# A second down block that begins with two plain pairs, and squares that discard into PSUM banks

## The chip, the cores and the metric

The kernel runs on one core of one Trainium2 chip. The metric is the device time of one execution in microseconds: median of 3 runs before the change 1084.82 (1084.63 to 1085.21).

## The reference

A decoder layer on x of 256 tokens by 2048, all in fp32, and a final norm:

```python
u = rmsnorm(h, ln1_w[l])
proj = jnp.einsum('bsd,de->bse', u, w_in[l])
...
h = h + jnp.einsum('bse,ed->bsd', y, w_out[l])
u = rmsnorm(h, ln2_w[l])
ff = jax.nn.silu(jnp.einsum('bsd,df->bsf', u, w_ffn_gate[l])) * jnp.einsum('bsd,df->bsf', u, w_ffn_up[l])
h = h + jnp.einsum('bsf,fd->bsd', ff, w_ffn_down[l])
return rmsnorm(h, final_norm_w)
```

`y` holds the outputs of a gated linear recurrence (convolution, scan) and of a chunkwise retention. The last product, `ff` (256 x 5632) by `w_ffn_down` (5632 x 2048), and the norm behind it are where the change lies.

## The kernel before

**Products.** Every fp32 number is split into a high part and a low part in the format fp32r, and each product of two blocks is three matmuls (`three`, L683 to L685): high by high, high of the left by low of the right, low of the left by high of the right. In names a trailing `h` or `l` is the part: `ah`, `al` are the left operand (activations), `sh`, `sl` sums of activation blocks, `wh`, `wl` and `bh`, `bl` weights (1024 wide and 512 wide).

**Weights.** A piece of 128 x 1024 fp32 (512 KB) is loaded by SyncE (L641) into one of 7 buffers named `raw`. `split` then makes two instructions: ScalarE (ACT) casts it (`wh`, L123), VectorE (DVE) subtracts (`wl`, L124). The 1024-wide results go to 4 pairs of split buffers, the 512-wide ones to the pool of 60 activation tiles [128 x 512] (`act_tile`), which also holds `ah`, `al`, intermediate `part`, `n` and, in the kernel before, `junk`. A buffer is free again when its last reader is done.

**Pairs.** The product is tiled in blocks of 256 tokens by 1024 columns (two halves of 128 tokens, two halves of 512 columns: banks `c11`, `c12`, `c21`, `c22` of PSUM). The inner dimension runs in pairs of two 128-row pieces. A *plain* pair (`EIGHT`) has 8 products, 24 matmuls of 512 columns. A *summed* pair (`SEVEN`) has 7 products, 21 matmuls, into `c11`, `c12`, `c21` and the banks `p1`, `p5`, `p6`, `p7`; it needs four sums of weight pieces, which DVE adds in place (`add`, L661). A summed pair's weights come in this order: the 512-wide `bh`, `bl` of the first piece; the second piece 1024 wide; then, after L661, the first load's buffer as (`t1`, `t3`), and the second's as (`t2`, `t4`). I write 12S for a summed pair 12.

**Two down blocks.** The columns 0 to 1023 are the first down block (d = 0), 1024 to 2047 the second (d = 1), each with 22 pairs in the order of `ORDER_DOWN`; `SUMMED_DOWN` says which are summed. The last two pairs of the second block (20 and 21) are split into 512-wide `bh`, `bl`, and their products are ordered by bank (`tail`): one of `c22b`, then `c11`, `c12`, `c21`, the left half of `c22`, the rest of `c22b`. When the last product of a bank is issued, `post` runs: `p1` is copied (ACT, L930); after `p7` DVE makes `n`, `part` and four updates of the rows `htok` (L934, L923, L924); a finished `c` bank is added to its row (DVE, L945), and `down_post` (L976) squares the row on ACT with a running sum (L983), and DVE multiplies it by the norm's weight (L988). L962 and L967 add the row of the last bank into PSUM ahead of its end.

**Order.** A scheduler that estimates each instruction's time fixes the order on each engine when the program is built; on the chip an engine goes strictly down its list. TensorE's order in the tail of the second down block is written by hand (L676 on, `manual_schedule`). Loads run three pairs ahead. When the sums of pairs 12 and 19 are no longer read, GpSimd loads the rows of the second block's columns back (`rows_back`, L1119).

## Time and profile before

| | |
|---|---|
| median of the runs | 1084.82 us |
| profiled execution | 1085.53 us |
| its span | 1083.7 us |
| TensorE busy | 1072.3 us, 99% |
| DVE, ACT busy | 972.0 us, 666.9 us |
| second down block begins | 958.21 us |
| last matmul begins | 1075.61 us |

The span is the profiled execution without what lies around it. In the profile PE is TensorE, and a matmul of 512 columns is shown with a length of 0.39 us but issues every 0.227 us, since matmuls overlap. A row of the timeline reads: start, length, engine, line, operation, output, inputs, size, and in brackets the idle time of the engine just before, with what ended it. In a table by stretch the number ahead of the DMA share is the TensorE clock granted, as a share of full speed.

### The profile page before, as it was taken

What the parts mean: (1) busy time and instruction counts of PE and PEld (TensorE: products, weight loads), DVE (VectorE), ACT (ScalarE), POOL (GpSimd) and SP (SyncE); (2) the same over time, 40 slices, a digit from 0 to 9 for tenths busy, and PEclk for the clock granted to TensorE, in tenths of its full rate; (3) what the DMA queues carried; (4) which work ended last, traced back from release to release, by engine and by line L of the source; (5) the groups of instructions that cost most, each with busy time, mean ns of one, the idle gap of its engine ahead of it and who ended that gap; (6) DMA issues with size and microseconds to landing.
All of it is one profiled execution on the core that took longest, in us unless ns stands there. A gap on an engine that the chain in (4) does not pass through costs nothing.

```text
span 1083.7 us, 14591 instructions
## 1 busy us (share of the span) xinstructions
PE 1072.3 (99%) x5083; PEld 897.5 (83%) x5083; DVE 972.0 (90%) x1411; ACT 666.9 (62%) x951; POOL 56.5 (5%) x73
## 2 busy tenths in 40 slices
PE   9999999999999999999999999999999999999997
PEld 7888888888888888888888888888888888878886
DVE  7789889988878889989999999999999899999886
ACT  7756744468746676656656566565656666655463
POOL 0603230000000000000000000000000010000001
PEclk9999999999999999999999999999999999999998
DMA  9964574554557587677776777776777856557662
GB/s 328 351 211 154 176 252 168 181 176 165 185 194 236 188 306 277 227 242 247 257 269 229 250 262 238 265 269 227 251 249 228 273 170 219 194 174 240 208 214 78
DMA packets 71386, 244.62 MB, mean 226 GB/s; under 512 B 8208, under 2 KB 8592, under 8 KB 71312
## 3 DMA queue, kind: packets, MB, share of 16 engines
q1 hardware_dynamic: 68400, 236.34, 64.3%
q0 software_dynamic: 1472, 4.72, 1.3%
q10 hardware_dynamic: 1440, 2.62, 0.6%
q8 instruction: 40, 0.66, 0.2%
q14 instruction: 34, 0.28, 0.1%
HBM read 239.46 MB, written 4.19 MB: 225 GB/s over the span
## 4 chain that ended last, share of the span: by engine, by line
PE 94%; POOL 1%; DMA 1%; DVE 1%; issue 1%; ACT 1%; SPq 0%; POOLq 0%; ACTq 0%
PE c L683 22%; PE c L685 22%; PE c L684 22%; PE fm L194 10%; PE fm L196 5%; PE tm L174 2%; PE tm L176 2%; PE tm L175 2%; PE p L685 1%; PE p L684 1%; PE p L683 1%; POOL sumsq L310 1%; PE ft L868 1%; DMA raw<-in_w_lx 1%; DMA raw<-in_w_v 0%
## 5 line engine op out<-in xcount | busy, mean ns | idle before, releaser
L123 ACT CAST wh<-raw 128x1024 fp32r<-128x1024 f32 (+1 forms) x500 | 464.5, 960 | 321.6 <-PE c L685 127.3
L124 DVE TENSOR_TENSOR wl<-raw,wh 128x1024 fp32r<-128x1024 f32 (+1 forms) x500 | 543.1, 1114 | 73.0 <-ACT wh L123 71.2
L684 PE MATMUL c<-wl,ah 128*128 128x512 f32 x814 | 317.7, 390 | 0.0
L685 PE MATMUL c<-wh,al 128*128 128x512 f32 x814 | 314.9, 389 | 0.0
L683 PE MATMUL c<-wh,ah 128*128 128x512 f32 x814 | 276.8, 392 | 0.0
L683 PEld LDWEIGHTS c<-wh,ah 128*128 128x128 f32 x814 | 153.4, 188 | 31.8 <-ACT wh L123 0.3
L685 PEld LDWEIGHTS c<-wh,al 128*128 128x128 f32 x814 | 152.8, 188 | 31.7 <-DVE al L124 0.3
L684 PEld LDWEIGHTS c<-wl,ah 128*128 128x128 f32 x814 | 152.9, 188 | 31.3
L194 PE MATMUL fm<-u,wh 128*128 128x512 f32 x512 | 161.3, 396 | 0.0
L196 PEld LDWEIGHTS fm<-u,wl 128*128 128x128 f32 x512 | 96.0, 188 | 22.5
L196 PE MATMUL fm<-u,wl 128*128 128x256 f32 x512 | 100.9, 278 | 0.0
L661 DVE TENSOR_TENSOR raw<-raw,raw 128x512 f32<-128x512 f32 x118 | 81.1, 688 | 2.0
L661 DVE TENSOR_TENSOR raw<-raw 128x512 f32<-128x512 f32 x118 | 80.6, 686 | 1.1
L194 PEld LDWEIGHTS fm<-u,wh 128*128 128x128 f32 x512 | 78.3, 189 | 0.3
L684 PE MATMUL c<-wl,sh 128*128 128x512 f32 x194 | 75.2, 389 | 0.0
L685 PE MATMUL c<-wh,sl 128*128 128x512 f32 x194 | 74.0, 389 | 0.0
L683 PE MATMUL c<-wh,sh 128*128 128x512 f32 x194 | 68.7, 391 | 0.3 <-ACT sh L123 0.3
L175 PE MATMUL tm<-wl,u 128*128 128x512 f32 x128 | 48.8, 394 | 0.0
L176 PE MATMUL tm<-wh,u 128*128 128x512 f32 x128 | 48.5, 390 | 0.0
L174 PE MATMUL tm<-wh,u 128*128 128x512 f32 x128 | 47.1, 398 | 0.8 <-ACT u L298 0.8
L1119 POOL DMA_DIRECT2D htok<-kept_rows x8 | 4.3, 546 | 796.4 <-DVE wl L124 704.0
L683 PEld LDWEIGHTS c<-wh,sh 128*128 128x128 f32 x194 | 36.4, 188 | 8.2 <-ACT sh L123 0.7
(247 smaller groups left out, 1076.2 us busy)
## 6 DMA issues: line engine op xcount, KB each, us to landing
raw<-in_w_gu SPq DMA_DIRECT2D x216, 512.0 KB, 5.1
raw<-in_w_down SPq DMA_DIRECT2D x91, 512.0 KB, 4.8
raw<-in_w_out SPq DMA_DIRECT2D x34, 512.0 KB, 4.3
raw<-in_w_lx SPq DMA_DIRECT2D x16, 512.0 KB, 6.9
raw<-in_w_k SPq DMA_DIRECT2D x16, 512.0 KB, 3.5
raw<-in_w_q SPq DMA_DIRECT2D x16, 512.0 KB, 3.7
raw<-in_w_rg SPq DMA_DIRECT2D x16, 512.0 KB, 3.5
raw<-in_w_lg SPq DMA_DIRECT2D x16, 512.0 KB, 3.4
```

Source lines behind the costliest of these rows:

```text
L123: act.copy(out=dst_h, in_=src)
L124: v.tensor_tensor(out=dst_l, in0=src, in1=dst_h.bitcast(F32), op=ALU.subtract)
L174: pe.matmul(ps, ah, wh, start=first, stop=False)
L175: pe.matmul(ps, ah, wl, start=False, stop=False)
L176: pe.matmul(ps, al, wh, start=False, stop=last)
L194: pe.matmul(ps, wh, hl, start=n + i == 0, stop=False)
L196: pe.matmul(ps[:, :S], wl, hl[:, :S], start=False, stop=n + i == len(order) - 1)
L310: pool.tensor_tensor(out=sumsq, in0=sumsq, in1=sq, op=ALU.add)
L661: v.tensor_tensor(out=dst, in0=a, in1=b, op=ALU.add)
L683: pe.matmul(p, ah, bh, start=first, stop=False, skip_group_check=onto)
L684: pe.matmul(p, ah, bl, start=False, stop=False, skip_group_check=onto)
L685: pe.matmul(p, al, bh, start=False, stop=last, skip_group_check=onto)
```

## The change

Two edits. The four squares of the first down block no longer write to an activation tile: `down_post` gets the bank that L945 has just read (`gone`), and the square's values, which nothing reads (only the sum beside them is used), are written there. The second block's order now starts with two plain pairs, 0 and 1, and from the third place on every other pair is summed until 17S: before it was summed at every other place from the second. What is computed, and the number of instructions of each engine, stay as they were.

```diff
-ORDER_DOWN = (3, 4, 0, 5, 6, 1, 7, 8, 2) + tuple(range(9, 22)), (0, 12, 1, 19, 2, 5, 3, 7, 4, 9, 6, 11, 8, 13, 10, 15, 14, 17, 16, 18, 20, 21)
+ORDER_DOWN = (3, 4, 0, 5, 6, 1, 7, 8, 2) + tuple(range(9, 22)), (0, 1, 12, 2, 19, 3, 5, 4, 7, 6, 9, 8, 11, 10, 13, 14, 15, 16, 17, 18, 20, 21)
...
-                    down_post(cb, t, 0, 512)
+                    down_post(cb, t, 0, 512, gone=None if d else ps[c])
...
-    def down_post(cb, t, c0, cw, src=None):
+    def down_post(cb, t, c0, cw, src=None, gone=None):
...
-        j = act_tile("junk")
+        j = act_tile("junk") if gone is None else gone
         act.activation(out=j[:, :cw], in_=src, func=AF.Square, accum_out=ssq[:, t, n : n + 1])
```

With it the order on the engines changes from the second down block on, at three places that matter here. In all rows a name's last numbers count the tiles.

**ACT where the second down block begins.** Before: the cast of 12S's second piece (`wh_1967`), a square, the cast of its (`t1`, `t3`), three squares, the `bh` of 19S, the cast of 12S's (`t2`, `t4`), then pair 1.

```order
L123 CAST bh_1960_9165<-raw_1959_9163 128x512
L123 CAST wh_1967_9231<-raw_1966_9229 128x1024
L983 ACTIVATE junk_1962_9182,ssq_120<-htok_1826_8628 128x512
L123 CAST wh_1969_9239<-raw_1959_9163 128x1024
L983 ACTIVATE junk_1963_9197,ssq_120<-htok_1828_8632 128x512
L983 ACTIVATE junk_1964_9212,ssq_120<-htok_1827_8630 128x512
L983 ACTIVATE junk_1965_9227,ssq_120<-htok_1829_8634 128x512
L123 CAST bh_1984_9289<-raw_1983_9287 128x512
L123 CAST wh_1971_9243<-raw_1966_9229 128x1024
L123 CAST wh_1974_9249<-raw_1973_9247 128x1024
```

Now: the casts of pair 1, three squares into the banks, the cast of 12S's second piece, the last square, the `bh` of 19S, then 12S's (`t1`, `t3`) and (`t2`, `t4`).

```order
L123 CAST bh_1966_9233<-raw_1965_9231 128x512
L123 CAST wh_1960_9165<-raw_1959_9163 128x1024
L123 CAST wh_1963_9227<-raw_1962_9225 128x1024
L983 ACTIVATE c11_1665_7913,ssq_120<-htok_1826_8628 128x512
L983 ACTIVATE c12_1668_7925,ssq_120<-htok_1828_8632 128x512
L983 ACTIVATE c21_1667_7921,ssq_120<-htok_1827_8630 128x512
L123 CAST wh_1973_9267<-raw_1972_9265 128x1024
L983 ACTIVATE c22_1666_7917,ssq_120<-htok_1829_8634 128x512
L123 CAST bh_1986_9321<-raw_1985_9319 128x512
L123 CAST wh_1975_9275<-raw_1965_9231 128x1024
L123 CAST wh_1977_9279<-raw_1972_9265 128x1024
```

The squares moved behind pair 1's casts, write PSUM banks, and 12S comes one plain pair later.

**DVE at the same place, now**, from the low parts of pair 1's second piece on (the next two instructions are `wl` of (`t1`, `t3`) and the L661 that completes `raw_1972`):

```order
L124 TENSOR_TENSOR wl_1964_9228<-raw_1962_9225,wh_1963_9227 128x1024
L988 TENSOR_TENSOR htok_1826_8628<-htok_1826_8628,fw_1830_8639 128x512
L988 TENSOR_TENSOR htok_1828_8632<-htok_1828_8632,fw_1831_8641 128x512
L661 TENSOR_TENSOR raw_1965_9231<-raw_1965_9231 128x512
L988 TENSOR_TENSOR htok_1827_8630<-htok_1827_8630,fw_1830_8639 128x512
L124 TENSOR_TENSOR wl_1974_9268<-raw_1972_9265,wh_1973_9267 128x1024
L988 TENSOR_TENSOR htok_1829_8634<-htok_1829_8634,fw_1831_8641 128x512
L124 TENSOR_TENSOR bl_1987_9322<-raw_1985_9319,bh_1986_9321 128x512
L661 TENSOR_TENSOR raw_1965_9231<-raw_1965_9231,raw_1972_9265 128x512
L661 TENSOR_TENSOR raw_1985_9319<-raw_1985_9319 128x512
L661 TENSOR_TENSOR raw_1972_9265<-raw_1965_9231,raw_1972_9265 128x512
L661 TENSOR_TENSOR raw_1985_9319<-raw_1985_9319,raw_1992_9350 128x512
```

Before, 12S's first three L661 came ahead of all L988; now L988 stands between them.

**DVE and PE in the tail.** Before, DVE had the low parts of the last two pairs (eight `bl`) and L967 in this order:

```order
L124 TENSOR_TENSOR bl_2132_10005<-raw_2130_10002,bh_2131_10004 128x512
L124 TENSOR_TENSOR bl_2134_10009<-raw_2130_10002,bh_2133_10008 128x512
L124 TENSOR_TENSOR bl_2137_10039<-raw_2135_10036,bh_2136_10038 128x512
L124 TENSOR_TENSOR bl_2139_10043<-raw_2135_10036,bh_2138_10042 128x512
L924 TENSOR_TENSOR htok_2041_9571<-htok_2041_9571,part_2126_9990 128x512
L124 TENSOR_TENSOR bl_2142_10049<-raw_2140_10046,bh_2141_10048 128x512
L124 TENSOR_TENSOR bl_2144_10053<-raw_2140_10046,bh_2143_10052 128x512
L124 TENSOR_TENSOR bl_2147_10084<-raw_2145_10081,bh_2146_10083 128x512
L124 TENSOR_TENSOR bl_2149_10088<-raw_2145_10081,bh_2148_10087 128x512
L967 TENSOR_TENSOR c22_1978_9261<-c22_1978_9261,htok_2041_9571 128x512
```

Now there are the low parts of 17S's (`t2`, `t4`), two of pair 18, and `n`:

```order
L124 TENSOR_TENSOR wl_2114_9948<-raw_2108_9933,wh_2113_9947 128x1024
L124 TENSOR_TENSOR wl_2117_9954<-raw_2115_9951,wh_2116_9953 128x1024
L124 TENSOR_TENSOR wl_2120_9984<-raw_2118_9981,wh_2119_9983 128x1024
L934 TENSOR_TENSOR n_2127_10018<-p6_1990_9339,part_2126_10000 128x512
L923 TENSOR_TENSOR part_2128_10020<-n_2127_10018,p5_1989_9335 128x512
```

Four row updates later come these, and then L962:

```order
L923 TENSOR_TENSOR part_2130_10026<-part_2129_10023,p5_1989_9335 128x512
L124 TENSOR_TENSOR bl_2133_10035<-raw_2131_10032,bh_2132_10034 128x512
L124 TENSOR_TENSOR bl_2135_10039<-raw_2131_10032,bh_2134_10038 128x512
L924 TENSOR_TENSOR htok_2037_9570<-htok_2037_9570,part_2130_10026 128x512
L124 TENSOR_TENSOR bl_2138_10045<-raw_2136_10042,bh_2137_10044 128x512
L124 TENSOR_TENSOR bl_2140_10049<-raw_2136_10042,bh_2139_10048 128x512
L124 TENSOR_TENSOR bl_2143_10080<-raw_2141_10077,bh_2142_10079 128x512
L967 TENSOR_TENSOR c22_1970_9245<-c22_1970_9245,htok_2037_9570 128x512
L124 TENSOR_TENSOR bl_2145_10084<-raw_2141_10077,bh_2144_10083 128x512
```

Two of the eight `bl` (`bl_2123`, `bl_2125`) are done earlier, ahead of 17S's last parts; the other six now stand behind `n` and the row updates of 17S, and the last one also behind L967. On PE `c22b`'s first product moved up into 17S, and the tail begins with `c11` alone:

```order
L685 MATMUL c21_1971_9249<-wh_2119_9983,al_1911_8965 128x512
L683 MATMUL c11_1968_9237<-bh_2122_9989,ah_1933_9062 128x512
L684 MATMUL c11_1968_9237<-bl_2123_9990,ah_1933_9062 128x512
L685 MATMUL c11_1968_9237<-bh_2122_9989,al_1934_9063 128x512
L683 MATMUL c11_1968_9237<-bh_2134_10038,ah_1933_9062 128x512
L684 MATMUL c11_1968_9237<-bl_2135_10039,ah_1933_9062 128x512
L685 MATMUL c11_1968_9237<-bh_2134_10038,al_1934_9063 128x512
L683 MATMUL c11_1968_9237<-bh_2137_10044,ah_1941_9102 128x512
L684 MATMUL c11_1968_9237<-bl_2138_10045,ah_1941_9102 128x512
L685 MATMUL c11_1968_9237<-bh_2137_10044,al_1942_9103 128x512
L683 MATMUL c11_1968_9237<-bh_2144_10083,ah_1941_9102 128x512
L684 MATMUL c11_1968_9237<-bl_2145_10084,ah_1941_9102 128x512
```

Before, `c22b` came first in it:

```order
L685 MATMUL c21_1979_9265<-wh_2128_9998,al_1911_8965 128x512
L683 MATMUL c22b_2150_10093<-bh_2133_10008,ah_1933_9062 128x256
L684 MATMUL c22b_2150_10093<-bl_2134_10009,ah_1933_9062 128x256
L685 MATMUL c22b_2150_10093<-bh_2133_10008,al_1934_9063 128x256
L683 MATMUL c11_1976_9253<-bh_2131_10004,ah_1933_9062 128x512
L684 MATMUL c11_1976_9253<-bl_2132_10005,ah_1933_9062 128x512
L685 MATMUL c11_1976_9253<-bh_2131_10004,al_1934_9063 128x512
L683 MATMUL c11_1976_9253<-bh_2138_10042,ah_1933_9062 128x512
L684 MATMUL c11_1976_9253<-bl_2139_10043,ah_1933_9062 128x512
L685 MATMUL c11_1976_9253<-bh_2138_10042,al_1934_9063 128x512
```

From 17S's first use of its (`t2`, `t4`) low part to the use of `bl_2145` are 35 matmuls in the program now: four of 17S, 21 of pair 18, ten of the tail.

## The prediction

> **What bounds the kernel now.** I read the page first: the busy shares, then the chain that ended last.

> ```profile
> PE 1072.3 (99%) x5083; PEld 897.5 (83%) x5083; DVE 972.0 (90%) x1411; ACT 666.9 (62%) x951; POOL 56.5 (5%) x73
> PE 94%; POOL 1%; DMA 1%; DVE 1%; issue 1%; ACT 1%; SPq 0%; POOLq 0%; ACTq 0%
> ```

> TensorE sets the end. Both programs issue the same 5031 matmuls, so only time in which PE waits, or runs at a lower clock, can change. The second view is the waits of PE over the whole run (engine, line, what it waited for; total, times, longest):

> ```profile
> PE warm L116 <- DVE eps_t L109: 1.1, 1, 1.1
> PE tm L174 <- ACT u L298: 0.8, 1, 0.8
> PE p L684 <- DVE wl L124: 0.8, 1, 0.8
> PE p L683 <- ACT wh L123: 0.5, 1, 0.5
> PE c L683 <- ACT sh L123: 0.3, 1, 0.3
> ```

> The third is a table by stretch (PE, PEld, DVE, ACT, POOL busy; granted clock; DMA share; GB/s). Of the last 180 us before the end only one stretch loses anything, and the two `p` waits above lie in it.

> ```profile
> 940.00:960.00 20.00, 20.00 (x90) 16.56 (x89) 18.48 (x24) 8.85 (x9) 0.00 (x0) 1.00 0.72 246
> 960.00:980.00 20.00, 18.66 (x73) 14.40 (x72) 18.15 (x26) 10.64 (x18) 0.00 (x0) 0.91 0.39 126
> 980.00:1000.00 20.00, 20.00 (x90) 16.57 (x89) 18.14 (x21) 11.83 (x13) 2.12 (x4) 1.00 0.78 266
> ```

> The timeline of PE there (start, length, what; in brackets the idle time): the second down block begins at 958.21.

> ```profile
> 958.21 0.39 PE L683 MATMUL c<-wh,ah 128*128 128x512 f32 x1
> 965.69 0.39 PE L683 MATMUL p<-wh,sh 128*128 128x512 f32 x1
> 966.86 0.50 PE L684 MATMUL p<-wl,sh 128*128 128x512 f32 x1 [0.79 <-DVE wl L124]
> 968.65 1.00 PE L683 MATMUL p<-wh,sh 128*128 128x512 f32 x2 [0.45 <-ACT wh L123]
> 973.09 0.39 PE L684 MATMUL c<-wl,ah 128*128 128x512 f32 x1
> ```

> From 958.21 to 965.69 are 33 intervals: 0.2267 us each is the pace. From 965.69 to 973.09 are 16 intervals, 3.63 us at that pace; they took 7.40. **3.77 us are lost.** Four intervals end at 968.65: 2.96 − 0.91 = 2.05 lost until then, waiting; the other 1.72 is the clock, below. Who is late:

> ```profile
> 956.41 1.05 ACT L123 CAST wh<-raw 128x1024 fp32r<-128x1024 f32 x1 [0.59 <-PE c L685]
> 963.62 0.63 ACT L983 ACTIVATE junk<-htok 128x512 f32<-128x512 f32 x1 [6.16 <-PE c L684]
> 964.25 1.04 ACT L123 CAST wh<-raw 128x1024 fp32r<-128x1024 f32 x1
> 967.55 4.03 ACT L123 CAST wh<-raw 128x1024 fp32r<-128x1024 f32 x4
> 961.19 0.68 DVE L661 TENSOR_TENSOR raw<-raw 128x512 f32<-128x512 f32 x1
> 964.38 0.69 DVE L988 TENSOR_TENSOR htok<-htok,fw 128x512 f32<-128x512 f32 x1 [1.06 <-ACT junk L983]
> 965.59 1.22 DVE L124 TENSOR_TENSOR wl<-raw,wh 128x1024 fp32r<-128x1024 f32 x1
> ```

> ACT stood 6.16 us before the square of L983, waiting for PE: its output `junk` takes an activation tile that PE was still reading for pair 0. The casts of 12S (S marks a summed pair) queue behind it, and DVE's L988 and `wl` behind those. PE starved on exactly these.

> **The clock.** The granted clock fell with the wait:

> ```profile
> 968.00:969.00 1.00, 0.55 (x2) 0.30 (x2) 1.00 (x3) 1.00 (x2) 0.00 (x0) 0.96 0.95 352
> 969.00:970.00 1.00, 1.00 (x4) 0.79 (x3) 1.00 (x2) 1.00 (x2) 0.00 (x0) 0.50 0.29 115
> 972.00:973.00 1.00, 1.00 (x5) 0.85 (x4) 1.00 (x2) 0.00 (x0) 0.00 (x0) 0.83 0.88 287
> 1078.00:1079.00 1.00, 0.00 (x0) 0.00 (x0) 0.90 (x3) 0.97 (x2) 0.00 (x0) 0.58 0.61 213
> 8.00:9.00 1.00, 0.82 (x4) 0.34 (x2) 0.00 (x0) 0.56 (x1) 0.00 (x0) 1.00 0.69 221
> 9.00:10.00 1.00, 0.35 (x2) 0.31 (x3) 0.91 (x3) 0.96 (x4) 0.00 (x0) 1.00 0.86 283
> ```

> A clock of 0.96 over one microsecond that is either full or half means half from 968.92; 0.83 means full again from 972.34. So 3.42 us ran at half speed: 1.71 us of PE work lost, which with the 2.05 makes up the 3.77. After the last matmul the clock falls at 1078.16, 109.24 us later, which is 32 × 3.414: I take it that the clock is decided at fixed steps of about 3.41 us. The step before 968.92, with 2.05 idle, brought half clock; 0.18 + 0.65 = 0.83 idle at 8 to 10 us did not.

> **The change, part by part.** *The squares.* They now write the PSUM bank that L945 has just read; DVE and ACT order is kept by waits, and the next block's `p1`, `p5` to `p7` need banks first after two plain pairs, 48 × 0.2267 = 10.9 us in, when the squares (four of 0.63) are long done; that work covers them. PSUM as ACT's output costs no more, by the groups of lines (busy, mean ns):

> ```profile
> L811 ACT COPY c<-q 128x512 f32<-128x512 f32 x13 | 7.6, 586 | 7.0 <-DVE q L810 7.0
> L808 ACT COPY p<-c 128x512 f32<-128x512 f32 x13 | 7.5, 576 | 1.6 <-PE c L685 1.6
> ```

> 586 into PSUM against 576 out of it. Term: 0.

> *The new beginning.* Pairs 0 and 1 are plain and PE reads them for 10.9 us. DVE works without a wait from 961.19: three 1024-wide `wl` and ten 512-wide operations stand before the L661 that releases the cast of 12S's last weights (t2, t4). Their pace comes from rows quoted next: (3.50 − 1.22)/2 = 1.14 and (2.49 − 0.68)/3 = 0.60. So that L661 starts at 961.19 + 3.42 + 6.03 = 970.64, takes 0.69, ACT follows 0.13 later (964.25 to 964.38 above is such a handover), and PE can use the cast 1.10 after its start (967.55 to 968.65): 972.56. PE asks for it at 958.21 + 63 × 0.2267 = 972.49. Loss 0.07. **Saved: 3.70.** If ACT or DVE loses a microsecond there, PE loses it too; the cover is thin.

> *The tail.* One plain pair fewer follows the last summed pair, 17S. The rows:

> ```profile
> 1030.99 4.63 DVE L124 TENSOR_TENSOR wl<-raw,wh 128x1024 fp32r<-128x1024 f32 x4 [0.59 <-ACT wh L123]
> 1041.72 3.50 DVE L124 TENSOR_TENSOR wl<-raw,wh 128x1024 fp32r<-128x1024 f32 x3 [0.60 <-ACT wh L123]
> 1062.90 2.49 DVE L124 TENSOR_TENSOR bl<-raw,bh 128x512 fp32r<-128x512 f32 x4
> 1065.31 0.69 DVE L967 TENSOR_TENSOR c<-c,htok 128x512 f32<-128x512 f32 x1
> 1067.97 0.69 DVE L945 TENSOR_TENSOR htok<-c,htok 128x512 f32<-128x512 f32 x1 [1.10 <-PE c L685]
> 1044.05 0.39 PE L684 MATMUL p<-wl,sh 128*128 128x512 f32 x1
> 1064.67 0.28 PE L683 MATMUL c22b<-bh,ah 128*128 128x256 f32 x1
> 1064.79 0.28 PE L684 MATMUL c22b<-bl,ah 128*128 128x256 f32 x1
> 1067.32 0.39 PE L684 MATMUL c<-bl,ah 128*128 128x512 f32 x1
> 1067.55 0.39 PE L685 MATMUL c<-bh,al 128*128 128x512 f32 x1
> ```

> Now: the last `bl` starts at 1062.90 + 1.81 = 1064.71. A 1024-wide `wl` started at 965.59 is used at 966.86, 1.27 later, so a 512-wide one 1.27 − 0.54 = 0.73 later: 1065.44. PE asks for it at 1067.32: 1.88 early.

> After: call N the moment when PE uses 17S's t2 (`p6`, L684). DVE prepared that weight a lead earlier than needed. In the kernel before, 15S has 1041.72 + 1.27 = 1042.99 against 1044.05: lead 1.06. To 17S DVE needs another round like 1030.99 to 1041.72, 10.73 (same rows of work: four `wl`, `bl`, and so on), while PE has 42 × 0.2267 + 3 × 0.12 = 9.88, since c22b's first product moved in there. Lead at 17S: 0.21, and nothing hides the rest. Then DVE does, in this order: `wl` of 17S, two `wl` of pair 18, `n`, five row updates, two `bl`, one more update, three `bl`, L967, the last `bl`. `n` starts at N − 1.27 − lead + 3 × 1.14 = N + 2.15 − lead; 13 × 0.60 later comes the last `bl`, ready 0.73 after that: N + 10.68 − lead. PE asks for it 35 intervals after N: 7.93. **Wait: 2.75 − lead, 2.5 with 0.21.** Bounds: 2.75 at lead 0; below, `n` can't start before `p6` is complete, 0.23 + 0.42 (1067.55 to 1067.97) after N, which leaves 0.65 + 7.80 + 0.73 − 7.93 = 1.25. I take 2.5, next to the row. It falls in three pieces: the second and fourth `bl` come late too, then the last one, which has L967 ahead of it, about 1.7.

> *Half clock after it.* That wait lies within 4 us, its largest piece in one step. The idle share of a step is thus about 1.7, between 0.83 (no loss) and 2.05 (loss), nearer to the latter. I take the loss, 1.71; other end 0.

> [...]

> **Sum**: −3.70 + 2.5 + 1.71 = +0.51, and 1085.53 becomes 1086.04. What follows PE's last product (row updates, norm, stores) is the same work in the same order and only shifts. The median of the runs, 1084.82, is 0.71 below the profiled run: **1085.3**.

> **Rivals.**
> *A, clock stays at full speed after the tail's wait*: 1085.3 − 1.7 = 1083.6. For it: no piece is longer than about 1.7. Against it: 968 to 972.
> *B is the forecast.*
> *C, the tail waits less*: DVE reaches 17S early, so only the 1.25 remains, too little for the clock: −2.45, 1082.4; with no wait at all 1081.1. For it: 15S's lead of 1.06 and 1.88 us of slack now. Against it: the order of DVE's work in the program.
> *D, slower: the supply of weights starves PE all through the block.* A summed and a plain pair cost PE 45 × 0.2267 = 10.20, DVE's round 10.73, since a load waits for the `wl` that frees its buffer. With 0.5 short in each of eight rounds, and 1.06 of lead to spend, 3.2 are lost, and the lead at 17S is 0: −3.70 + 3.2 + 2.75 + 1.71 = +4.0, 1088.8. It decides from the point at which the starving costs over 1.7. Against it: the kernel before runs the same rounds with a lead of 1.06 left at the seventh.
> *E, the change doesn't do what it says*: another item in ACT's queue (19S's `bh`, which takes pair 0's tile) holds it up as the square did; 1085.3 + 3.7 = 1089.0. Its cast stands ahead of 12S's t-casts, but pair 0's tile is free at about 963.6, before DVE gets that far.

> **Chances**: B 0.46, A 0.26, C 0.16, D 0.10, E 0.02. A measurement of this kernel can tell about 0.2%, 2.2 us, from no change. C is faster (0.16, and a little of A: 0.17); A and B within; D, E and a little of B slower (0.13). B alone gives 1084.3 to 1085.9; the range from C's 1082.4 to 1086.8 (starving of 1.5) leaves out C's better half, most of D, and E, under 2 in 10.

> **What would show it.** PE's waits lose both `p` rows of before, and the clock row at 969 reads 1.00. New rows stand near 1062 to 1066, PE `c` L684 waiting for DVE `bl` L124, in pieces of 0.2 to 1.7, total 2.5; then the clock reads 0.50 for 3.4 us. If the tail shows no such wait, the order of DVE was misread; if `p` L683 waits in every round between 980 and 1055, D holds; if waits for ACT `wh` stay near 968, E.

## The result, and the profile after

The changed kernel takes 1086.57 us (median of 20 runs, 1084.93 to 1087.96) against 1084.86 (20 runs, 1083.69 to 1085.5): ratio 1.0017, 95% interval 1.001 to 1.0024, so slower by 0.1 to 0.24%. The forecast was 1085.3, range 1082.4 to 1086.8. The time lies within, near the upper end; the way there was in part another than forecast.

The profiled execution took 1086.56 us, span 1084.8. Both profiles hold 5083 matmuls (the prediction's 5031 is in neither). PE's waits over the whole run, those of the second down block:

```profile
PE c L684 <- DVE bl L124: 1.7, 2, 1.4
...
PE p L683 <- ACT wh L123: 0.6, 1, 0.6
...
PE c L683 <- ACT wh L123: 0.4, 2, 0.2
```

Both waits of before at the block's beginning are gone. In their place stand waits for `bl` (the tail) and new ones for `wh`. The table by stretch says where:

```profile
960.00:980.00 20.00, 20.00 (x89) 16.31 (x88) 18.71 (x24) 9.56 (x14) 0.00 (x0) 1.00 0.48 154
...
1000.00:1020.00 20.00, 19.79 (x87) 15.65 (x86) 16.11 (x18) 9.43 (x11) 0.00 (x0) 1.00 0.58 186
1020.00:1040.00 20.00, 19.15 (x81) 14.61 (x80) 17.12 (x20) 10.88 (x12) 0.00 (x0) 1.00 0.53 182
...
1060.00:1080.00 20.00, 15.37 (x74) 11.99 (x72) 16.23 (x39) 8.27 (x21) 4.15 (x5) 1.00 0.15 53
```

960 to 980 loses no busy time now (before 1.34, and clock 0.91). 1000 to 1040 does, where before PE was busy throughout, as these two rows of the kernel before show:

```profile
1000.00:1020.00 20.00, 20.00 (x90) 16.56 (x89) 17.41 (x20) 10.27 (x12) 0.00 (x0) 1.00 0.60 192
1020.00:1040.00 20.00, 20.00 (x90) 16.55 (x89) 16.61 (x19) 10.54 (x12) 0.00 (x0) 1.00 0.61 206
```

Now the clock reads 1.00 in every one of these stretches, in the tail too. PE's timeline at the block's ends and at the pieces that cost, in the changed kernel:

```profile
957.47 0.39 PE L683 MATMUL c<-wh,ah 128*128 128x512 f32 x1
...
971.84 0.73 PE L683 MATMUL p<-wh,sh 128*128 128x512 f32 x2
...
1004.17 0.96 PE L683 MATMUL c<-wh,ah 128*128 128x512 f32 x3 [0.21 <-ACT wh L123]
...
1025.44 0.50 PE L683 MATMUL p<-wh,sh 128*128 128x512 f32 x1 [0.56 <-ACT wh L123]
...
1026.39 0.96 PE L683 MATMUL c<-wh,ah 128*128 128x512 f32 x3 [0.21 <-ACT wh L123]
...
1065.90 0.50 PE L684 MATMUL c<-bl,ah 128*128 128x512 f32 x1 [0.24 <-DVE bl L124]
...
1068.31 0.50 PE L684 MATMUL c<-bl,ah 128*128 128x512 f32 x1 [1.44 <-DVE bl L124]
...
1076.77 0.28 PE L685 MATMUL c22b<-bh,al 128*128 128x256 f32 x1
```

From the block's first product to its last are 512 intervals. Before they took 1075.61 − 958.21 = 117.40 us, of which 3.76 is lost against the pace; now 1076.77 − 957.47 = 119.30, of which 5.66 is lost. Laying each start against the pace of 0.2267 us gives the pieces: 0.2 at the beginning (971.8 to 972.4), 2.5 in the tail (1064.7 to 1068.7), and 3.0 in the rounds between, of which 1.6 near 1025. So the block lost 1.90 us more than before. In this execution it also began 0.74 us earlier, from differences at the very start of the run; hence the end is only 1.16 later in the two profiles, while the medians differ by 1.71.

### The profile page after: what moved, and what is told of

It is laid out like the page before. It is cut to its first block, busy times and chain, and to the rows that moved or that the text cites. A ratio compares the mean times of both kernels' runs of the same rounds, so it can differ in the third digit from the quotient of the medians.

```text
span 1084.8 us, 14590 instructions
## 1 busy us (share of the span) xinstructions
PE 1072.3 (99%) x5083; PEld 895.0 (83%) x5083; DVE 972.4 (90%) x1411; ACT 666.3 (61%) x951; POOL 55.8 (5%) x73
## 4 chain that ended last, share of the span: by engine, by line
PE 87%; DVE 5%; DMA 4%; ACT 2%; POOL 1%; issue 1%; SPq 0%; ACTq 0%; POOLq 0%; DVEq 0%
PE c L685 20%; PE c L684 20%; PE c L683 20%; PE fm L194 10%; PE fm L196 5%; DMA raw<-in_w_down 3%; PE tm L174 3%; PE tm L176 3%; PE tm L175 3%; DVE wl L124 2%; DVE raw L661 2%; POOL sumsq L310 1%; PE ft L868 1%; ACT wh L123 1%; DVE bl L124 1%
## 5 line engine op out<-in xcount | busy, mean ns | idle before, releaser
L123 ACT CAST wh<-raw 128x1024 fp32r<-128x1024 f32 (+1 forms) x500 | 463.4, 960 | 320.1 <-PE c L685 116.2
L124 DVE TENSOR_TENSOR wl<-raw,wh 128x1024 fp32r<-128x1024 f32 (+1 forms) x500 | 543.5, 1116 | 70.5 <-ACT wh L123 69.0
L684 PE MATMUL c<-wl,ah 128*128 128x512 f32 x814 | 317.7, 390 | 0.0
L685 PE MATMUL c<-wh,al 128*128 128x512 f32 x814 | 314.9, 389 | 0.0
L683 PE MATMUL c<-wh,ah 128*128 128x512 f32 x814 | 276.3, 392 | 0.5 <-ACT wh L123 0.4
L683 PEld LDWEIGHTS c<-wh,ah 128*128 128x128 f32 x814 | 152.3, 188 | 33.5 <-ACT wh L123 2.6
L685 PEld LDWEIGHTS c<-wh,al 128*128 128x128 f32 x814 | 152.8, 188 | 31.8 <-DVE al L124 0.3
L684 PEld LDWEIGHTS c<-wl,ah 128*128 128x128 f32 x814 | 152.8, 188 | 31.4
L661 DVE TENSOR_TENSOR raw<-raw,raw 128x512 f32<-128x512 f32 x118 | 81.1, 688 | 1.9
L661 DVE TENSOR_TENSOR raw<-raw 128x512 f32<-128x512 f32 x118 | 80.8, 687 | 1.1
L684 PE MATMUL c<-wl,sh 128*128 128x512 f32 x194 | 75.2, 389 | 0.0
L685 PE MATMUL c<-wh,sl 128*128 128x512 f32 x194 | 74.0, 389 | 0.0
L683 PE MATMUL c<-wh,sh 128*128 128x512 f32 x194 | 68.7, 391 | 0.3 <-ACT sh L123 0.3
L174 PE MATMUL tm<-wh,u 128*128 128x512 f32 x128 | 46.6, 394 | 0.6 <-ACT u L298 0.5
L683 PEld LDWEIGHTS c<-wh,sh 128*128 128x128 f32 x194 | 36.4, 188 | 8.2 <-ACT sh L123 0.7
```

What stands on the lines that cost most here:

```text
L123: act.copy(out=dst_h, in_=src)
L124: v.tensor_tensor(out=dst_l, in0=src, in1=dst_h.bitcast(F32), op=ALU.subtract)
L174: pe.matmul(ps, ah, wh, start=first, stop=False)
L661: v.tensor_tensor(out=dst, in0=a, in1=b, op=ALU.add)
L683: pe.matmul(p, ah, bh, start=first, stop=False, skip_group_check=onto)
L684: pe.matmul(p, ah, bl, start=False, stop=False, skip_group_check=onto)
```

## The experiments

**Which of the two edits does it?** `squares_only` has the first edit with the old order, `order_only` the second with activation tiles for the squares.

```diff
 squares_only, against the changed kernel:
-ORDER_DOWN = ..., (0, 1, 12, 2, 19, 3, 5, 4, 7, 6, 9, 8, 11, 10, 13, 14, 15, 16, 17, 18, 20, 21)
+ORDER_DOWN = ..., (0, 12, 1, 19, 2, 5, 3, 7, 4, 9, 6, 11, 8, 13, 10, 15, 14, 17, 16, 18, 20, 21)
 order_only, against the changed kernel:
-        j = act_tile("junk") if gone is None else gone
+        j = act_tile("junk")
```

> The first edit alone: the four squares discard into the PSUM banks, the order of the second down block is that of the kernel before. Theory (the order does the work): the 6.16 us wait of ACT before L983 goes, but 12S still follows after only one plain pair (24 products, 5.4 us), and DVE has the same row updates, low parts and sums to do before 12S's (t1, t3) and (t2, t4); PE still waits there, now for DVE, about 1.4 and 1.2 us in two pieces, and the rounds behind it start with no lead and starve by 0.3 us or more each. Time 1085 to 1088, not faster than before. Rival (the square's wait for a tile was the whole cause): the 3.77 us go and nothing comes, 1081.1.

> The second edit alone: the order with two plain pairs first, the squares still write activation tiles. Theory (the order does the work): with pair 1 after pair 0 the squares and casts find free tiles in time and PE loses 0.1 us at the boundary, as in the changed kernel; the tail's wait of 2.5 us and the starving of the rounds by about 2.7 us stay: 1086 to 1087.5, not told apart from the changed kernel. Rival (the square's tile is the cause): ACT waits again at L983, PE loses 2 to 3.8 us more, 1088.5 to 1090.5.

Measured: `squares_only` 1089.09 us, ratio 1.0044 (1.0031 to 1.0058); `order_only` 1086.46, ratio 1.0017 (1.0007 to 1.0026). PE's timeline in `squares_only`, and the cast that ended the second of these waits:

```profile
967.80 0.50 PE L684 MATMUL p<-wl,sh 128*128 128x512 f32 x1 [1.12 <-DVE wl L124]
969.53 0.91 PE L683 MATMUL p<-wh,sh 128*128 128x512 f32 x2 [1.00 <-ACT wh L123]
...
968.44 3.99 ACT L123 CAST wh<-raw 128x1024 fp32r<-128x1024 f32 x4 [2.49 <-DVE raw L661]
...
993.93 0.50 PE L683 MATMUL p<-wh,sh 128*128 128x512 f32 x1 [1.16 <-ACT wh L123]
```

The square's wait for a tile is gone in `squares_only`, and PE waits at the same place all the same, now for DVE's work: its `wl`, and its L661 ahead of the cast at 968.44. With the clock it loses 4.3 us against the pace there, and 2.0 more at 994. So the 3.77 us of before were not the square's alone: with one plain pair ahead of 12S there is not enough time for DVE. `order_only` can't be told from the changed kernel, and its profile loses only 0.5 us at the beginning: with two plain pairs first, the tiles for the squares are free in time. The order is the change; beside it the first edit is worth nothing measurable here, and alone it is a loss. For `squares_only` even the theory's range (1085 to 1088) was too low: it left out the clock, which halved behind that wait in the profiled execution, as in the profile of the kernel before (table by stretch of `squares_only`):

```profile
970.00:971.00 1.00, 1.00 (x4) 0.82 (x3) 1.00 (x2) 1.00 (x2) 0.00 (x0) 0.50 0.16 62
```

**The tail.** `pair17_plain` gives the tail a plain pair more by making pair 17 plain; `two_behind` takes the end of the old order, with 15S directly behind 13S.

```diff
 pair17_plain, against the changed kernel:
-SUMMED_DOWN = (9, 12, 15, 17, 19), (5, 7, 9, 11, 12, 13, 15, 17, 19)
+SUMMED_DOWN = (9, 12, 15, 17, 19), (5, 7, 9, 11, 12, 13, 15, 19)
 two_behind, against the changed kernel:
-... 10, 13, 14, 15, 16, 17, 18, 20, 21)
+... 10, 13, 15, 14, 17, 16, 18, 20, 21)
```

> The changed kernel with pair 17 plain instead of summed (one product more, 3 matmuls, 0.68 us; four sums of DVE fewer). Theory (the tail's wait comes of too little PE work behind the last summed pair's row updates): 15S is the last summed pair, with 16, 17 and 18 plain behind it, 72 matmuls, 16 us of cover; the waits for DVE bl, 2.5 us, go; the starving of the rounds up to 15S stays: 1086.5 - 2.5 + 0.7 = 1084.7, 1083.5 to 1085. Rival (the last pairs' loads or casts are late by themselves): the wait stays, 1087.2.

> The changed kernel with the end of the order of the kernel before (10, 13S, 15S, 14, 17S, 16, 18, 20, 21): two plain pairs again behind 17S, and in exchange 15S directly behind 13S. Theory: the waits for DVE bl (2.5 us) go; between 13S and 15S PE has 21 matmuls less cover (a plain pair is 5.4 us), so a new wait of 1 to 2 us for ACT wh stands near 1040; the starving before it stays: 1084.5 to 1086. Rival (the wait in the tail is not of the order): it stays, and the new wait adds to it, 1088.

Measured: `pair17_plain` 1084.1 us, ratio 0.9996 (0.9987 to 1.0005); `two_behind` 1086.34, ratio 1.0019 (1.001 to 1.0028). In neither is a wait for `bl` left. What `two_behind` gains in the tail it pays near 1040:

```profile
1042.11 0.50 PE L683 MATMUL p<-wh,sh 128*128 128x512 f32 x1 [1.74 <-ACT wh L123]
...
1043.05 0.96 PE L683 MATMUL c<-wh,ah 128*128 128x512 f32 x3 [0.22 <-ACT wh L123]
```

That is 2.5 us against the pace, above the 1 to 2 expected, and the time is 0.3 above the theory's range. Seven of the 11 runs have a mean clock of 0.996; the profiled one has 0.998, and its clock did not halve before PE's end. The tail's wait is DVE's list behind 17S, as the prediction had it: give PE a second plain pair behind the last summed pair and it goes.

**GpSimd for low parts.** If DVE's list is the matter, another engine could take some of it. In `pool_tail` GpSimd subtracts four of the last two pairs' eight `bl`; in `pool_b11` the first low part of every summed pair; in `pool_both` all of these.

```diff
 def split(dst_h, dst_l, src, by=None):
     act.copy(out=dst_h, in_=src)
-    v.tensor_tensor(out=dst_l, ...)
+    (by or v).tensor_tensor(out=dst_l, ...)
...
 pool_tail, pool_both: the second half of a load of the last two pairs
+    split(*self.parts[name], raw[:, n * 512 : n * 512 + 512], pool if n == 1 else None)
 pool_b11, pool_both: the first part of a summed pair of the second down block
+    split(*self.parts["b11"], r[:, :512], pool if self.last else None)
```

> The changed kernel with the second low part of each load of the last two pairs (four of the eight bl, the last one among them) subtracted by GpSimd instead of DVE. Theory (the tail's wait is DVE's list behind n): three operations of 0.60 us leave DVE's list ahead of PE's last need and the last bl no longer stands behind L967; the waits for DVE bl, 2.5 us with what they drag along, fall under 0.5, the starving of the rounds stays: 1083.5 to 1084.7. Rival (the wait is for the loads or the casts of the last pairs): no gain, 1086.6, or slower, since GpSimd takes about 1.3 us for what DVE does in 0.60.

> As pool_tail, and the first low part (b11) of every summed pair of the second down block is also made by GpSimd. Theory (the rounds starve because DVE's list holds the low part of the next summed pair, whose load is late, ahead of the sums and splits that PE needs first): DVE no longer stops for the load, its round falls from 10.6 us to 10.2 or less, the waits of PE for ACT wh between 1000 and 1040 go: 1081 to 1082.5, faster than both kernels. Rival (the loads or DVE's amount of work limit the round, wherever the low part stands): the waits stay, no better than pool_tail, 1083.5 to 1084.7.

> The changed kernel with the first low part of every summed pair of the second down block made by GpSimd, the tail left to DVE. In the two runs before, an all-SBUF operation of DVE took up to 2.1 us instead of 0.69 while GpSimd subtracted. Theory (starving comes of DVE stopping for the next summed pair's load; GpSimd gives part of it back by slowing DVE): the waits between 1000 and 1040 fall from 2.7 us to 1.0 to 1.5, the tail's 2.5 us stay: 1084.5 to 1086. Rival (nothing but the amount of DVE work or the loads counts): no less starving, 1086.5 or more.

Measured: `pool_tail` 1085.57 us, ratio 1.0015 (1.0006 to 1.0023); `pool_both` 1085.6, 1.0012 (1.0004 to 1.0021); `pool_b11` 1088.0, 1.0033 (1.0021 to 1.0044). All three are slower than their theories said. The timelines of GpSimd, DVE and PE in `pool_tail` say why:

```profile
1059.02 4.61 POOL L124 TENSOR_TENSOR bl<-raw,bh 128x512 fp32r<-128x512 f32 x3 [6.46 <-ACT bh L123]
...
1060.16 1.28 DVE L923 TENSOR_TENSOR part<-n,p 128x512 f32<-128x512 f32 x2
1061.37 2.81 DVE L924 TENSOR_TENSOR htok<-htok,part 128x512 f32<-128x512 f32 x2
...
1066.63 0.50 PE L684 MATMUL c<-bl,ah 128*128 128x512 f32 x1 [1.40 <-DVE bl L124]
```

While GpSimd subtracts (1059.02 to 1063.63), DVE's two L923, which read one operand from PSUM, take 1.28, as in the changed kernel; the two L924, both operands in SBUF, take 2.81 instead of the changed kernel's 1.29 and end at 1064.18, just after GpSimd does. DVE loses 1.5 of the 1.8 us that it was spared. In `pool_both` the same two pairs took 1.29 and 2.82.

`pool_b11` fails for a second reason: the first sum (L661) overwrites the piece that GpSimd still reads, and DVE waits for it instead of for the load:

```profile
1028.44 0.69 DVE L661 TENSOR_TENSOR raw<-raw,raw 128x512 f32<-128x512 f32 x1
1030.65 0.69 DVE L661 TENSOR_TENSOR raw<-raw 128x512 f32<-128x512 f32 x1 [1.52 <-POOL bl L124]
```

So it moved the stop of DVE but did not take it away. In its profile the loss between 1000 and 1060 did fall, from 2.9 us against the pace to 1.3, but half clock behind the tail's wait (below) takes as much again: the block loses 5.6 us in all, as in the changed kernel. Why the median is some 1.5 us above the changed kernel's is not explained by that.

**The rounds.** In the changed kernel, DVE and ACT ahead of the worst starving, at 1025:

```profile
1013.56 4.63 DVE L124 TENSOR_TENSOR wl<-raw,wh 128x1024 fp32r<-128x1024 f32 x4 [0.60 <-ACT wh L123]
1020.60 0.69 DVE L124 TENSOR_TENSOR bl<-raw,bh 128x512 fp32r<-128x512 f32 x1 [2.40 <-ACT bh L123]
1025.42 4.63 DVE L124 TENSOR_TENSOR wl<-raw,wh 128x1024 fp32r<-128x1024 f32 x4 [0.58 <-ACT wh L123]
...
1035.98 1.22 DVE L124 TENSOR_TENSOR wl<-raw,wh 128x1024 fp32r<-128x1024 f32 x1 [0.59 <-ACT wh L123]
...
1019.94 0.62 ACT L123 CAST bh<-raw 128x512 fp32r<-128x512 f32 x1 [3.57 <-DMA raw<-in_w_down]
```

DVE stands 2.40 us before a `bl`, ACT 3.57 before its cast, for a load. This `bl` belongs to the *next* summed pair: it stands a round ahead of its use, and behind it in DVE's list stand the sums and splits of the present pair, which PE needs first. The load itself was issued at 1014.82, when the first `wl`, begun at 1013.56, had freed its buffer. From `wl` to `wl` the loop takes 11.86 us here and 10.56 in the following round, while PE needs 10.20.

The loop follows this one load: by their issues and landings in the trace the loads issued at 1004.46, 1014.82, 1026.67 and 1037.23 took 3.60, 5.10, 3.81 and 3.48 us, and the rounds 10.36, 11.86, 10.56 and 10.23, each 6.76 or 6.75 more. So, by these four rounds, a load above 3.44 (10.20 − 6.76) makes DVE's round longer than PE's. The longest round lies ahead of these, 12.64 us from the `wl` at 990.56 to the one at 1003.20:

```profile
998.37 0.69 DVE L124 TENSOR_TENSOR bl<-raw,bh 128x512 fp32r<-128x512 f32 x1 [3.19 <-ACT bh L123]
...
1003.20 4.63 DVE L124 TENSOR_TENSOR wl<-raw,wh 128x1024 fp32r<-128x1024 f32 x4 [0.59 <-ACT wh L123]
```

Its load, issued at 991.80, took 5.89 us, and the four transfers of `rows_back` were under way until 994.79. The kernel before has them at the same place (until 993.78), and its load of 991.12 took 5.13, but there one more `wl` and a sum stood ahead of that `bl`, and DVE did not stop for it. Whether `rows_back` makes this load late was not tested.

To test whether that `bl`'s place in the list causes the starving, `tied` adds a made-up dependency that keeps that `bl` behind this pair's sums: it costs two operations of one column per round, 0.15 us each in its profile. `tied_two_behind` adds an order with two plain pairs at both ends and the two adjacent summed pairs (9, 11) in the middle; `tied_old_order` is the old order with squares in banks.

```diff
 in load(), first half of a summed pair of the second down block:
+                if self.last and tie:
+                    v.tensor_tensor(out=r[:, :1], in0=r[:, :1], in1=tie[0], op=ALU.add)
                 split(*self.parts["b11"], r[:, :512])
...
 in add(), behind the four sums:
+            if self.last:
+                tie[:] = [m3[:, :1]]
+                v.tensor_tensor(out=tie[0], in0=b21[:, :1], in1=b21[:, :1], op=ALU.subtract)
...
 tied_two_behind, besides:
+ORDER_DOWN = ..., (0, 1, 12, 2, 19, 3, 5, 4, 7, 6, 9, 11, 8, 13, 10, 15, 14, 17, 16, 18, 20, 21)
```

> The changed kernel with a made-up dependency: a DVE operation of one column behind each summed pair's last sum gives a zero, and another adds it to the first column of the next load to be split as b11; so the scheduler can't put the low part of the next summed pair ahead of the sums of this one. Two operations of one column (about 0.1 to 0.2 us each) per round are added. Theory (the rounds starve because DVE's list stops there for a load that is requested only one round before): the waits between 1000 and 1040, 2.2 to 2.7 us in all runs of this order, fall under 0.3; with the lead regained 17S comes early enough that the tail's wait shrinks from 2.5 to its floor, 1.3 to 1.6: 1082.5 to 1083.7. Rival (the loads themselves or DVE's amount of work limit the round): the waits stay, and 3 us of added operations make it 1086.5 or more.

> As tied, with pair 11 directly behind pair 9 (both summed) in the middle of the block and two plain pairs behind 17S again. Theory: with the rounds free of the load, DVE gains up to 1.5 us on PE per round, so by 9S it has the lead that two summed pairs in a row cost, a wait of 0.5 us near 1018 remains, and the tail's wait goes: all three losses of the changed kernel but 0.5 us are gone, 1081 to 1082, faster than both kernels. Rival (two summed pairs in a row cost what they cost in two_behind): a wait of 2 us near 1018, 1083.

> Squares in the banks and the made-up dependency, in the order of the kernel before (one plain pair first). Theory: the block's beginning stays short of DVE time with one plain pair ahead of 12S, PE waits about 1.7 us there (0.4 and 1.3), and whether the clock falls after it differs from run to run; the rounds and the tail lose nothing: 1082.5 to 1084.5. Rival (as in squares_only, the loss of the first round is handed on): waits in every round, 1087 or more.

Measured: `tied` 1083.38 us (1082.88 to 1083.64), ratio 0.9988 (0.9979 to 0.9997); `tied_two_behind` 1082.5 (1081.77 to 1082.75), ratio 0.9979 (0.9971 to 0.9988); `tied_old_order` 1083.39 (1083.25 to 1083.77), ratio 0.9991 (0.9982 to 1.0). `tied`, by PE's waits and the table by stretch (its lines stand six further down, L690 is L684):

```profile
PE c L690 <- DVE bl L124: 1.2, 1, 1.2
...
1000.00:1020.00 20.00, 20.00 (x90) 16.57 (x89) 19.10 (x25) 11.62 (x12) 0.00 (x0) 1.00 0.63 211
1020.00:1040.00 20.00, 20.00 (x90) 16.57 (x89) 17.65 (x24) 11.37 (x12) 0.00 (x0) 1.00 0.65 211
```

No round starves, though DVE does slightly more. The tail's wait shrank to one piece, 1.5 us against the pace, near the lower bound of the prediction (1.25). In `tied_two_behind` the list of PE's waits over the whole run has none for weights left in the second down block:

```profile
PE warm L116 <- DVE eps_t L109: 1.1, 1, 1.1
PE tm L174 <- ACT u L298: 0.8, 2, 0.6
PE c L689 <- ACT sh L123: 0.3, 1, 0.3
```

Against the pace it loses 0.4 us, near 1017, where 0.5 was expected. It is faster than the kernel before by 0.21%, and than the changed kernel by about 3.8 us when each is set against its own runs of the kernel before; the time is a little above the 1081 to 1082 expected. And `tied_old_order` shows that with the rounds freed the first order loses only its beginning, 1.8 us (PE's timeline):

```profile
965.57 0.50 PE L689 MATMUL p<-wh,sh 128*128 128x512 f32 x1 [0.24 <-ACT wh L123]
967.02 0.74 PE L689 MATMUL p<-wh,sh 128*128 128x512 f32 x2 [0.95 <-ACT wh L123]
```

The spread of runs fell with it: 0.8, 1.0 and 0.5 us for these three, 3.0 for the changed kernel (20 runs, these 10 or 11). A loop that waits for a load hands on the load's variation, as the four rounds above show within one execution; that this is what spread the runs is not shown.

**The clock.** Why did it stay? `longer_gap` puts one more DVE operation into the tail.

```diff
 behind L967
+                v.tensor_tensor(out=act_tile("more"), in0=htok[3, 1], in1=htok[3, 1], op=ALU.add)
```

> The changed kernel with one more DVE operation (512 wide, 0.60 us, its result unused) behind L967 in the tail, ahead of the last bl. Theory (the clock falls when a step of 3.41 us holds more idle time than a threshold between 1.7 and 2.05 us): PE's last wait grows from 1.6 to 2.2 us, and in the profile, if the wait lies within one step, the granted clock then reads 0.50 for 3.4 us: 1086.5 + 0.6 + 1.7 = 1088.8; where the wait straddles two steps, only +0.6, so the runs spread over 1086.5 to 1090. Rival (the clock falls only behind a single pause near a whole step): +0.6 alone, 1087.1, clock at 1.00 until PE ends.

Measured: 1087.42 us (1085.59 to 1088.22), ratio 1.0021 (1.0012 to 1.0031). PE's row and the table by stretch:

```profile
1068.06 0.80 PE L684 MATMUL c<-bl,ah 128*128 128x512 f32 x1 [2.04 <-DVE bl L124]
...
1067.00:1068.00 1.00, 0.00 (x0) 0.00 (x0) 1.00 (x3) 0.20 (x1) 0.00 (x0) 0.88 0.00 0
1068.00:1069.00 1.00, 0.94 (x2) 0.83 (x3) 0.34 (x2) 0.00 (x0) 0.00 (x0) 0.50 0.00 0
...
1071.00:1072.00 1.00, 1.00 (x5) 0.78 (x5) 0.14 (x1) 1.00 (x1) 1.00 (x1) 0.92 0.00 0
```

The clock reads half from 1067.76 to 1071.16, 3.40 us, and meanwhile PE's matmuls start 0.43 us apart (1068.65 to 1070.79 for five), as in the kernel before (969.44 to 971.58), against 0.227. At that pace 3.41 us cost 1.6; the prediction's 1.71 took half speed for it. That the clock is decided at fixed steps of 3.41 us is the prediction's estimate, from 3.42 us at half clock and the 109.24 us between two falls. By it the step before the fall, 1064.35 to 1067.76, held 0.41 + 1.91 = 2.3 us of idle time, counting the waits alone. In `pool_b11` it halves at 1067.90 (0.95 over a microsecond), after a step with 0.36 + 1.59 = 1.95, from its own two waits in the tail:

```profile
1064.85 0.50 PE L684 MATMUL c<-bl,ah 128*128 128x512 f32 x1 [0.24 <-DVE bl L124]
1067.25 0.50 PE L684 MATMUL c<-bl,ah 128*128 128x512 f32 x1 [1.43 <-DVE bl L124]
...
1067.00:1068.00 1.00, 0.75 (x3) 0.66 (x4) 0.54 (x2) 0.01 (x1) 0.00 (x0) 0.95 0.00 0
```

In the changed kernel the clock doesn't halve there:

```profile
1068.00:1069.00 1.00, 0.69 (x3) 0.59 (x4) 0.59 (x2) 0.07 (x1) 0.00 (x0) 1.00 0.00 0
...
1080.00:1081.00 1.00, 0.00 (x0) 0.00 (x0) 0.06 (x1) 0.13 (x1) 0.00 (x0) 0.56 0.87 315
```

It falls at 1080.12 there, behind the end; three and four estimated steps of 3.414 earlier are 1069.88 and 1066.46, and the step between these holds the whole last wait, 1.61. So, with steps estimated in this way, 1.61 in one step left the clock up and 1.95 was followed by half clock. (Against the pace, with the 0.11 us that the first product behind each wait takes longer, it is 1.72 and 2.2.) The rival (only a pause near a whole step counts) is refuted: the clock halved behind pauses of 1.6 (`pool_b11`) and 2.2 us, each with one of 0.4 ahead of it. The median of `longer_gap` is only 0.85 above the changed kernel's, less than the theory's 2.3: seven of its ten runs have a mean clock of 0.996 or 0.997 (1087.15 to 1088.22 us), three have 0.998 (1085.59 to 1086.64), which reads as if the clock did not halve in all. That the cause is where the steps fall in each run is an estimate; no run shows it. The changed kernel's runs differ in the same way: of its 20 runs the five with a mean clock of 0.996 or 0.997 took 1086.87 to 1087.96, median 1087.65, the others 1084.93 to 1087.29, median 1086.51.

## Why the prediction was right or wrong

- **The boundary: right for the profiled execution.** Forecast saved 3.70; the loss there went from 3.76 to 0.2, so 3.5. The weak point named (12S's cast just in time, 0.07) measured 0.2. The cause as told was incomplete: behind the square's wait stood another, and `squares_only` shows that one, DVE's. And about 1.6 of the 3.70 is the halved clock, which most runs of the kernel before do not seem to have had. The profiles in which the clock halved ahead of PE's end have a mean clock of 0.996 or 0.997 (that of before 0.996), the others 0.997 to 0.999. Of the 83 runs of the kernel before that were taken beside the experiments, 16 have 0.996, with a median of 1085.35 us, and 54 have 0.998 or 0.999, with 1084.36. The prediction took the 0.71 between profile and median as a constant; so that the change saves 3.70, or 3.5, in the median is not shown.
- **The tail's wait: right**, in place, cause and size: 2.5 forecast, 2.5 measured, its last piece 1.6 against "about 1.7". The order on DVE and the durations of before were enough for it. (The lead at 17S was 0.5, not 0.21: the weight was ready at 1057.49 and used at 1057.99.)
- **Half clock after it: wrong.** The term +1.71 was not there in the profiled run nor, by their mean clock, in about 15 of 20. The step that failed is the guess that 1.7 of idle in one step is "nearer to the latter" of 0.83 and 2.05. Case A was right here. What stood for it, that no piece is longer than about 1.7, settles nothing alone: `pool_b11` halved behind pieces of 0.36 and 1.59. 1.61 against 1.95 is a close call; that some runs fell on the other side is an estimate from the five mean clocks of 0.996 and 0.997.
- **The rounds: wrong.** The sum set starving at 0, and rival D, with 3.2 us and a chance of 0.10, was what happened: 3.0. The row against D, a lead of 1.06 at 15S in the kernel before, was misread. DVE's round of 10.73 against PE's 10.20 was in the rows, so that lead was being used up; it must have been built up earlier. Where the changed kernel lost it stays open. PE's stall of 3.77 at the beginning of before, which gave loads and DVE time, is one possible source; against it stands `squares_only`, where PE lost 4.3 at the beginning and starved at 994 all the same. The rows name another, the round of 12.64 beside `rows_back`. Shown is that the place of that `bl`, which makes DVE wait for the load, causes the starving (`tied`). Nor did the rounds lose evenly, as D had it: 1.6 of the 3.0 fell near 1025, behind one load of 5.10.
- **The sum was near by chance**: −3.70 + 2.5 + 1.71 = +0.5 stood for −3.5 + 2.5 + 3.0 + 0 = about +1.9 in the two profiles. One term of 1.7 too much stood against one of 3.0 left out. What makes up the 1.71 between the medians is not known piece by piece, since one profile per kernel was taken and the clock differs from run to run. D and A together were the true case, and they had been weighed as if only one could come.

## What to carry to other kernels

A wait that is removed may take with it the slack that it gave to everything behind it: before counting its whole length as a gain, compare the round of each supplying loop with the round of the engine that sets the end, and treat a loop that is longer as a cost, whatever lead it shows now. A profile is one execution: before a loss of it, such as a halved clock, goes into a forecast of the median, see from the other runs how often it occurs. In a list that is worked off in order, as DVE's was here (it stood 2.40 us for one load), look for an instruction whose input is a transfer and which stands ahead of work that is already ready; a tiny dependency that moves it may be worth more than a new order of the whole. And where a block of supply-heavy work is moved, look at both its ends: here, cover gained at the beginning was taken from the tail.
